# Gate and up weights in 1 MB pieces with 8 KB rows, and three transposing steps moved behind the modulation's sums, in a decoder block with 64 experts

## The chip, the cores and the metric

The kernel runs on one core of one Trainium2 chip. The metric is device time in microseconds from one launch. Three runs of the kernel before took 740.38, 738.90 and 739.66 us, median 739.66. A core has a matrix engine (TensorE, PE in the profile; PEld is its loading of the stationary operand), a vector engine (DVE), a scalar engine for activations (ACT), GpSimd (POOL), a queue engine (SP) that here issues nearly all loads, and 16 DMA engines that carry them from the chip's memory into the core's buffers.

## The reference, cut to what matters

One layer on 256 tokens of 1024 channels: modulation, two attention branches, then a mixture of 64 experts (8 for each token) and a shared expert, and a final norm. The parts that the change touches are the first modulation and the experts:

```python
mod = jax.nn.silu(c) @ w_ada[l] + b_ada[l]
shift1, scale1, gate1, shift2, scale2, gate2 = jnp.split(mod, N_MOD, axis=-1)
h = modulate(rms_norm(x, norm1_g[l]), shift1, scale1)
proj = h @ w_in[l]
...
def swiglu(x, w_gate, w_up, w_down):
    return (jax.nn.silu(x @ w_gate) * (x @ w_up)) @ w_down
...
def body(acc, bidx):                      # for every block of rows of one expert
    ye = swiglu(xt[rows], w_gate_e[e], w_up_e[e], w_down_e[e]) * wr[:, None]
    return acc.at[rows].add(ye.astype(acc.dtype)), None
...
return routed + swiglu(xt, w_gate_sh, w_up_sh, w_down_sh)
```

All is in 32 bit floats. An expert's gate and up matrices are 1024 x 256 (1 MiB each), its down matrix 256 x 1024 (1 MiB). All 64 experts are read: 192 MiB, which is 201 of the 266.73 MB that move.

## The kernel before

**Stages.** First the modulation row is summed (`mod_sums`, one step for each eighth of the channels, on TensorE, as its 1 MB of `w_ada` lands), and the normed tokens are turned so that channels lie on partitions (`turned`, four transposes of 128 x 128 a step, two channel blocks for both token tiles). `shift_scale` copies the sums out of PSUM on ScalarE, turns them into columns with four small products, and VectorE adds the biases. `modulated` makes the two parts (high and rest) of the modulated activations, `row_hi` and `row_lo` the two parts of the weights, and `proj_row` multiplies. Projections, both attentions and the output projection follow, then the router, and then the expert tiles.

**Expert tiles.** The experts are sorted by their number of tokens; the first six have fixed places. A tile has 128 slots: two experts of 64, one of 96 and one of 32, or four of 32. There are 26 tiles, 20 with two experts and 6 with four. For a tile TensorE gathers the tokens (`gather`), multiplies with gate and up weights (`tile_up`: the experts of a tile stand in column groups of the array, and their products run side by side), makes the slot map, adds the previous tile's result to the sums (`scatter`), turns the hidden activations and multiplies with the down weights (`down`). `swiglu` runs on ScalarE and VectorE meanwhile. Every product of 32 bit floats appears as two records in the trace.

**Weights.** They land in a ring of 20 buffers of 1 MiB (`w8()`; the names `w`, `vv`, `whi`, `wlo`, `hh`, `g2r`, `gr`, `sr`, `xs` in the rows are its buffers, most of them taken over from the attention stage). A buffer is handed out again when the tile that used it last is through with it. Loads are issued in program order by one queue on SP, which stops at a load whose buffer is not free or when earlier loads still have to land. In `load_gu` one buffer holds four of the eight channel blocks, gate and up of each: two loads of 512 KB, each row 4 KB. A tile loads the first half of all its experts and then the second. A down matrix is one load of 1 MB with 8 KB rows. The last tile's second halves come in pieces of 256 KB with 2 KB rows, and its down matrices in cuts of 512, 256 and 256 columns.

**Order.** The engines' programs are written out by hand (`plan`, `do`), so the order on every engine is that of the code.

Of the kernel before, what the change touches and what calls it, by code (L numbers as in the profile page):

```python
# [9 lines left out]
F32 = mybir.dt.float32  # L10
# [15 lines left out]
FF = 256  # L26
# [82 lines left out]
def block_kernel(ctx: ExitStack, tc: tile.TileContext, x, c, norm1_g, norm2_g, w_ada, b_ada, w_in,  # L109
                 w_branch_sb, w_branch_mb, w_out, w_router, router_bias, w_gate_e, w_up_e, w_down_e,  # L110
                 w_gate_sh, w_up_sh, w_down_sh, rel_bias, final_g, const_a, const_m, const_b, out):
    nc = tc.nc
# [47 lines left out]
    def load_gu(wg, wu, h):  # L160
        w = w8().rearrange("p (g j f) -> p g j f", g=2, j=4)
        nc.sync.dma_start(w[:, 0], wg.rearrange("(p j) f -> p j f", j=8)[:, 4 * h:4 * h + 4])
        nc.sync.dma_start(w[:, 1], wu.rearrange("(p j) f -> p j f", j=8)[:, 4 * h:4 * h + 4])
        return [w[:, :, j, :] for j in range(4)]
# [38 lines left out]
    with ExitStack() as pa:  # L203
# [158 lines left out]

        def shift_scale():

            sb = wk.tile([P, 512], F32, name="adasb", tag="ada", bufs=2)
            nc.scalar.activation(sb, rows.pop("m"), AF.Copy)
            p = big()
            firsts = ident.rearrange("p (n r) -> p n r", r=32)[:, :, 0]
            for k in range(4):
                mm(p[:, 4 * k:4 * k + 4], sb[:, 128 * k:128 * k + 128], firsts, start=True, stop=True,  # L370
                   skip_group_check=True)
            p = p[:, 0:16].rearrange("p (k i u) -> p i u k", k=4, i=2)
            m = modq.rearrange("p (u k) i -> p u k i", u=2)
            bq = biasq.rearrange("p (u k) i -> p u k i", u=2)
            nc.vector.tensor_tensor(m[:, :, :, 1], p[:, 0], bq[:, :, :, 1], op=OP.add)
            nc.vector.tensor_tensor(m[:, :, :, 0], p[:, 1], bq[:, :, :, 0], op=OP.add)
            nc.vector.tensor_tensor(modq[:, :, 2], modq[:, :, 0], gb[:, 0:8], op=OP.mult)
# [321 lines left out]
        for j in range(3, 8):  # L699
            if j > 3:  # L700
                do(turned, 2 * j - 8)
            do(mod_sums, j, keys=[("adk", j)])
        do(shift_scale)
        do(modulated, 0)
# [250 lines left out]
    def late_expert(k):  # L955
# [9 lines left out]
        gu = load_gu(wg, wu, 0) + load_gu(wg, wu, 1)  # L965
        wd = load_dn(wd)
        for first in (0, 128):
# [16 lines left out]
            for j in range(8):  # L984
                mm(p, xg[:, j], gu[j], start=j == 0, stop=j == 7)
# [5 lines left out]
    def load_shared():  # L991
        shw["gu"] = load_gu(w_gate_sh[0], w_up_sh[0], 0) + load_gu(w_gate_sh[0], w_up_sh[0], 1)
# [14 lines left out]
    def shared_up(t, j0, j1):  # L1007
        if j0 == 0:
            shp[t] = rot() if t else gub()
        for j in range(j0, j1):  # L1010
            mm(shp[t], h2T[0][:, j, t * 128:(t + 1) * 128], shw["gu"][j], start=j == 0, stop=j == 7)
# [76 lines left out]
    def load_tile(i):  # L1088
# [8 lines left out]
        if i == len(TILES) - 1:  # L1097

            gu = [load_gu(e[0], e[1], 0) for e in es]
            ws = [w8().rearrange("p (g j f) -> p g j f", g=2, j=4) for e in es]  # L1100
            for j in (0, 2):
                for w, e in zip(ws, es):
                    for g in range(2):
                        nc.sync.dma_start(w[:, g, j:j + 2],
                                          e[g].rearrange("(p j) f -> p j f", j=8)[:, 4 + j:6 + j])
            for g, w in zip(gu, ws):
                g += [w[:, :, j, :] for j in range(4)]
            return gu, load_dn_cuts([e[2] for e in es])
        gu = [[] for s in range(n)]
        for h in range(2):  # L1110
            for s in range(n):
                gu[s] += load_gu(es[s][0], es[s][1], h)
# [11 lines left out]
    def tile_up(i, xg, gu, between=()):  # L1124
        p = gub()
        for j in range(8):
            if j == 4:
                for f in between:
                    f()
            for c0, n, s in groups(i):  # L1130
                mm(p[c0:c0 + n, :], xg[:, j, c0:c0 + n], gu[s][j], start=j == 0, stop=j == 7, skip_group_check=True)  # L1131
# [203 lines left out]
```

## Time and profile before

| | |
|---|---|
| runs, median (three) | 739.66 us |
| profiled execution | 740.37 us, span of its instructions 738.6 us |
| TensorE busy | 691.3 us, 94% of the span |
| VectorE, ScalarE busy | 316.2 us (43%), 202.2 us (27%) |
| carried by DMA | 266.73 MB, mean 361 GB/s |
| gate and up loads | 512 KB each; down loads 1024 KB |

TensorE's records are pipelined, so a busy share of 94% does not say that it never waits: a wait shorter than a record's own length does not show as idle. The share of the DMA engines is the time their packets took over the time of 16 engines; it reads a little above 1 where every engine always has a packet, since one begins as the last ends. The chain of waits is followed back from the last instruction, so it shows for each stretch which resource ended last there. In the page's 40 slices the transfer rate is uneven until the fourteenth slice and then near 412 GB/s for most of the rest.

### The profile page before, as it was taken

To read this page: it belongs to the slowest core of one execution; us is meant where nothing else is said; L and a number is where in the kernel's file an instruction comes from. 1 tells how busy PE (TensorE), PEld (TensorE's weight loads), DVE (VectorE), ACT (ScalarE), POOL (GpSimd) and SP (SyncE) were. 2 spreads that over 40 slices of the span, in tenths; PEclk is the share of its full clock that TensorE was granted. 3 is DMA by queue.
4 is the path that set the end of the run, shared out by engine and by line. 5 is a ranking of instruction groups with operands and counts; after the bars stand their busy time and mean duration, and the time that the engine had idled before them with its cause. 6 is when DMAs were issued, how large, how long until landed. Compare 5 with 4: busy or idle time off the path is not lost.

```text
span 738.6 us, 12518 instructions
## 1 busy us (share of the span) xinstructions
PE 691.3 (94%) x4743; PEld 384.3 (52%) x4743; DVE 316.2 (43%) x667; ACT 202.2 (27%) x332; POOL 16.0 (2%) x33
## 2 busy tenths in 40 slices
PE   3899999999999999999999999999989998899994
PEld 0486677676888546444444454344444553355532
DVE  1366766666576833333333333233233332233323
ACT  2344666555835521111111111111111111111122
POOL 1010001000001000000000000000000000000000
PEclk9899999999999999999999999999999999999998
DMA  9999988777567699999999999999999999999994
GB/s 354 412 385 387 364 271 301 251 269 273 177 235 269 259 375 416 354 389 412 409 415 414 413 390 412 411 412 412 416 413 412 412 412 415 412 411 408 402 335 158
DMA packets 76862, 266.73 MB, mean 361 GB/s; under 512 B 7013, under 2 KB 9221, under 8 KB 67968
## 3 DMA queue, kind: packets, MB, share of 16 engines
q1 hardware_dynamic: 75344, 262.24, 91.7%
q0 software_dynamic: 1312, 3.65, 1.5%
q8 instruction: 39, 0.64, 0.4%
q14 instruction: 23, 0.19, 0.1%
q10 hardware_dynamic: 144, 0.00, 0.0%
HBM read 264.68 MB, written 1.19 MB: 360 GB/s over the span
## 4 chain that ended last, share of the span: by engine, by line
PE 51%; DMA 45%; DVE 2%; ACT 1%; issue 0%; SPq 0%; DVEq 0%; ACTq 0%
DMA w<-in_w_up_e_dram 17%; PE gu L1131 9%; PE big L272 7%; PE big L275 7%; PE big L273 7%; DMA wlo<-in_w_up_e_dram 7%; DMA sr<-in_w_down_e_dram 5%; PE rot L1155 4%; DMA w<-in_w_down_e_dram 4%; DMA hh<-in_w_down_e_dram 4%; DMA w<-in_w_ada_dram 4%; PE rot L1071 3%; DMA gr<-in_w_up_e_dram 3%; PE acc L1187 3%; PE att L420 2%; DMA hh<-in_w_gate_e_dram 2%
## 5 line engine op out<-in xcount | busy, mean ns | idle before, releaser
L1131 PE MATMUL gu<-w,hl 128*32 128x512 f32 (+1 forms) x568 | 99.0, 594 | 2.4 <-DMA w<-in_w_up_e_dram 2.0
L272 PE MATMUL big<-whi,hh 128*128 128x512 f32 x184 | 75.2, 409 | 1.7 <-ACT whi L392 1.7
L273 PE MATMUL big<-whi,hl 128*128 128x512 f32 x184 | 72.9, 396 | 0.0
L1004 DVE TENSOR_TENSOR sg<-sg,gu 128x256 f32<-128x256 f32 x27 | 11.4, 421 | 138.7 <-ACT sg L1003 138.7
L1071 PE MATMUL rot<-S,qksb 128*128 128x128 bf16 x624 | 69.1, 219 | 0.0
L1071 PE MATMUL rot<-S,qkmb 128*128 128x128 bf16 x624 | 68.7, 219 | 0.0
L1167 ACT ACTIVATE mg<-y 128x512 fp32r<-128x512 f32 x51 | 32.1, 629 | 130.2 <-DVE y L1161 130.2
L1161 DVE SCALAR_TENSOR_TENSOR y<-rot,wsl,gate 128x512 f32<-128x512 f32 (+1 forms) x53 | 39.1, 738 | 65.0 <-PE rot L1155 63.1
L1131 PEld LDWEIGHTS gu<-w,hl 128*32 128x32 f32 (+1 forms) x568 | 29.9, 121 | 60.9 <-issue 58.8
L1155 PE MATMUL rot<-w,at 128*32 128x512 f32 (+1 forms) x256 | 56.2, 610 | 5.7 <-DVE at L1019 5.7
L254 DVE TENSOR_TENSOR wlo<-w,whi 128x2048 fp32r<-128x2048 f32 x23 | 52.7, 2291 | 20.1 <-ACT whi L253 19.1
L275 PE MATMUL big<-wlo,hh 128*128 128x512 f32 x184 | 54.2, 395 | 0.2 <-DVE wlo L254 0.2
L1187 PE MATMUL acc<-mg,ST 128*128 128x512 f32 x204 | 54.0, 406 | 0.0
L1168 DVE TENSOR_TENSOR mg<-y,mg 128x512 fp32r<-128x512 f32 x51 | 35.3, 692 | 38.4 <-ACT mg L1167 38.4
L1075 ACT ACTIVATE hl<-rot 128x512 f32<-128x512 f32 x26 | 15.5, 597 | 120.8 <-PE rot L1071 120.8
L1003 ACT ACTIVATE sg<-gu 128x256 f32<-128x256 f32 x27 | 10.4, 383 | 138.5 <-PE gu L1131 138.5
L1071 PEld LDWEIGHTS <-qksb 128*128 128x128 bf16 x624 | 42.6, 98 | 7.8 <-issue 6.7
L1187 PEld LDWEIGHTS acc<-mg,ST 128*128 128x128 f32 x204 | 36.3, 188 | 17.4 <-ACT sg L1003 9.1
L253 ACT ACTIVATE whi<-w 128x2048 fp32r<-128x2048 f32 x23 | 43.9, 1909 | 5.0 <-PE big L273 5.0
L272 PEld LDWEIGHTS big<-whi,hh 128*128 128x128 f32 x184 | 35.1, 191 | 17.1 <-issue 3.8
L1071 PEld LDWEIGHTS <-qkmb 128*128 128x128 bf16 x624 | 43.6, 98 | 0.0
L275 PEld LDWEIGHTS big<-wlo,hh 128*128 128x128 f32 x184 | 34.8, 190 | 8.4 <-DVE wlo L254 0.6
(352 smaller groups left out, 1055.7 us busy)
## 6 DMA issues: line engine op xcount, KB each, us to landing
w<-in_w_gate_e_dram SPq DMA_DIRECT2D x60, 512.0 KB, 12.1
w<-in_w_up_e_dram SPq DMA_DIRECT2D x60, 512.0 KB, 12.6
w<-in_w_down_e_dram SPq DMA_DIRECT2D x26, 1024.0 KB, 12.5
w<-in_w_ada_dram SPq DMA_DIRECT2D x24, 1024.0 KB, 11.6
w<-in_w_in_dram SPq DMA_DIRECT2D x16, 1024.0 KB, 12.4
whi<-in_w_gate_e_dram SPq DMA_DIRECT2D x12, 512.0 KB, 11.3
whi<-in_w_up_e_dram SPq DMA_DIRECT2D x12, 512.0 KB, 11.7
wlo<-in_w_down_e_dram SPq DMA_DIRECT2D x6, 1024.0 KB, 11.3
```

Of the source, the lines that this page charges most:

```text
L253: nc.scalar.activation(hi, w, AF.Copy)
L254: nc.vector.tensor_tensor(lo, w, hi.bitcast(F32), op=OP.subtract)
L272: mm(p, aa[i][0], ww[i][0], start=start and i == 0, stop=False)
L273: mm(p, aa[i][1], ww[i][0], start=False, stop=False)
L275: mm(p, aa[i][0], ww[i][1], start=False, stop=stop and i == n - 1)
L1071: mm(p[:, b * 128:(b + 1) * 128], hp3[k // 3][k % 3][:, half * 4 + b, :], S[:, k // 3], start=k == 0, stop=k == 5)
L1131: mm(p[c0:c0 + n, :], xg[:, j, c0:c0 + n], gu[s][j], start=j == 0, stop=j == 7, skip_group_check=True)
L1155: mm(py[c0:c0 + w, 0:n], at[:, jj, c0:c0 + w], wd[s][:, jj, o:o + n], start=jj == 0, stop=jj == 1, skip_group_check=True)
L1161: nc.vector.scalar_tensor_tensor(y, py[:, 0:n], wsl, gate2[:, o:o + n], op0=OP.mult, op1=OP.mult)
L1167: nc.scalar.activation(yh, y, AF.Copy)
L1168: nc.vector.tensor_tensor(yl, y, yh.bitcast(F32), op=OP.subtract)
L1187: mm(sums(t, c), m if len(y) > 1 else m.bitcast(F32), part, start=False, stop=stop and k == len(y) - 1, skip_group_check=True)
```

## The change

Three edits. First, a gate matrix is one load of 1 MB into a buffer of its own and an up matrix another, each partition reading one row of 8 KB; a tile issues the gate loads of all its experts, then the up loads. In the last tile the up matrices come as 512, 256 and 256 KB. Second, the products follow: for every group first the eight gate products of 256 columns, then the eight up products (`up_cut`), where eight products of 512 columns stood. Third, at the front the steps `turned(2)`, `turned(4)` and `turned(6)` move from between the last sums to behind them, one beside the copy of the sums, two behind `shift_scale`; the copy is a step of its own (`mod_copy`).

```diff
-    def load_gu(wg, wu, h):
-        w = w8().rearrange("p (g j f) -> p g j f", g=2, j=4)
-        nc.sync.dma_start(w[:, 0], wg.rearrange("(p j) f -> p j f", j=8)[:, 4 * h:4 * h + 4])
-        nc.sync.dma_start(w[:, 1], wu.rearrange("(p j) f -> p j f", j=8)[:, 4 * h:4 * h + 4])
-        return [w[:, :, j, :] for j in range(4)]
+    def load_gu(wg, wu):
+
+        ws = [w8().rearrange("p (j f) -> p j f", j=8) for _ in range(2)]
+        for w, d in zip(ws, (wg, wu)):
+            nc.sync.dma_start(w, d.rearrange("(p j) f -> p j f", j=8))
+        return ws
+
+    def up_cut(p, xg, gu, gs, k):
+
+        g, j = divmod(k, 8)
+        for c0, n, s in gs:
+            mm(p[c0:c0 + n, FF * g:FF * g + FF], xg[:, j, c0:c0 + n], gu[s][g][:, j, :], start=j == 0, stop=j == 7,
+               skip_group_check=True)
...
+        def mod_copy():
+            sb = rows["c"] = wk.tile([P, 512], F32, name="adasb", tag="ada", bufs=2)
+            nc.scalar.activation(sb, rows.pop("m"), AF.Copy)
+
         def shift_scale():
 
-            sb = wk.tile([P, 512], F32, name="adasb", tag="ada", bufs=2)
-            nc.scalar.activation(sb, rows.pop("m"), AF.Copy)
-            p = big()
+            sb, p = rows.pop("c"), big()
...
         for j in range(3, 8):
-            if j > 3:
-                do(turned, 2 * j - 8)
+            if j == 4:
+                do(turned, 0)
             do(mod_sums, j, keys=[("adk", j)])
+
+        do(mod_copy)
+        do(turned, 2)
         do(shift_scale)
+        do(turned, 4)
+        do(turned, 6)
         do(modulated, 0)
...
-        for j in range(j0, j1):
-            mm(shp[t], h2T[0][:, j, t * 128:(t + 1) * 128], shw["gu"][j], start=j == 0, stop=j == 7)
+        for k in range(2 * j0, 2 * j1):
+            up_cut(shp[t], h2T[0][:, :, t * 128:(t + 1) * 128], [shw["gu"]], [(0, 128, 0)], k)
...
-            gu = [load_gu(e[0], e[1], 0) for e in es]
-            ws = [w8().rearrange("p (g j f) -> p g j f", g=2, j=4) for e in es]
-            for j in (0, 2):
-                for w, e in zip(ws, es):
-                    for g in range(2):
-                        nc.sync.dma_start(w[:, g, j:j + 2],
-                                          e[g].rearrange("(p j) f -> p j f", j=8)[:, 4 + j:6 + j])
-            for g, w in zip(gu, ws):
-                g += [w[:, :, j, :] for j in range(4)]
+            gu = [[w8().rearrange("p (j f) -> p j f", j=8) for g in range(2)] for e in es]
+            for g, o, m in ((0, 0, 8), (1, 0, 4), (1, 4, 2), (1, 6, 2)):
+                for w, e in zip(gu, es):
+                    nc.sync.dma_start(w[g][:, o:o + m], e[g].rearrange("(p j) f -> p j f", j=8)[:, o:o + m])
             return gu, load_dn_cuts([e[2] for e in es])
-        gu = [[] for s in range(n)]
-        for h in range(2):
-            for s in range(n):
-                gu[s] += load_gu(es[s][0], es[s][1], h)
+        gu = [[w8().rearrange("p (j f) -> p j f", j=8) for g in range(2)] for e in es]
+        for g in range(2):
+            for w, e in zip(gu, es):
+                nc.sync.dma_start(w[g], e[g].rearrange("(p j) f -> p j f", j=8))
         return gu, [load_dn(e[2]) for e in es]
...
         p = gub()
-        for j in range(8):
-            if j == 4:
+        for k in range(16):
+            if k == 8:
                 for f in between:
                     f()
-            for c0, n, s in groups(i):
-                mm(p[c0:c0 + n, :], xg[:, j, c0:c0 + n], gu[s][j], start=j == 0, stop=j == 7, skip_group_check=True)
+            up_cut(p, xg, gu, groups(i), k)
```

What the edits do to the order is read best from the engines' own programs. At the front, TensorE before: line 360 is a sum, line 351 a transposing step (`att<-ca,gr`), line 370 the products that turn the sums into columns, line 272 the first projection product.

```order
L360 MATMUL big<-w_112,cpad 32x512 x4
L351 MATMUL att<-ca,gr_102 128x128 x4
L360 MATMUL big<-w_114,cpad 32x512 x4
L351 MATMUL att<-ca,gr_102 128x128 x4
L360 MATMUL big<-w_116,cpad 32x512 x4
L351 MATMUL att<-ca,gr_102 128x128 x4
L360 MATMUL big<-w_118,cpad 32x512 x4
L351 MATMUL att<-ca,gr_102 128x128 x4
L360 MATMUL big<-w_125,cpad 32x512 x4
L370 MATMUL big<-ca,adasb 128x4 x4
L272 MATMUL big<-whi,hh 128x512
```

The same place on TensorE after the change (sums are line 368 now, steps 359, columns 380, products 280):

```order
L368 MATMUL big<-w_112,cpad 32x512 x4
L359 MATMUL att<-ca,gr_102 128x128 x4
L368 MATMUL big<-w_114,cpad 32x512 x4
L368 MATMUL big<-w_116,cpad 32x512 x4
L368 MATMUL big<-w_118,cpad 32x512 x4
L368 MATMUL big<-w_125,cpad 32x512 x4
L359 MATMUL att<-ca,gr_102 128x128 x4
L380 MATMUL big<-ca,adasb 128x4 x4
L359 MATMUL att<-ca,gr_102 128x128 x8
L280 MATMUL big<-whi,hh 128x512
```

The sums stand together now, one transposing step behind them and two behind the columns.

The loads' queue on SP at tile 2 before (two fixed experts; the name ahead of the arrow is the ring's buffer, and the order is hh, g2r, gr, gr):

```order
L162 DMA hh<-in_w_gate_e_dram 128x1024
L163 DMA hh<-in_w_up_e_dram 128x1024
L162 DMA g2r<-in_w_gate_e_dram 128x1024
L163 DMA g2r<-in_w_up_e_dram 128x1024
L162 DMA gr_2449<-in_w_gate_e_dram 128x1024
L163 DMA gr_2449<-in_w_up_e_dram 128x1024
L162 DMA gr_2452<-in_w_gate_e_dram 128x1024
L163 DMA gr_2452<-in_w_up_e_dram 128x1024
L168 DMA sr<-in_w_down_e_dram 128x2048
L168 DMA xs<-in_w_down_e_dram 128x2048
```

The same tile in SP's queue after:

```order
L1122 DMA hh<-in_w_gate_e_dram 128x2048
L1122 DMA gr_2483<-in_w_gate_e_dram 128x2048
L1122 DMA g2r<-in_w_up_e_dram 128x2048
L1122 DMA gr_2484<-in_w_up_e_dram 128x2048
L176 DMA sr<-in_w_down_e_dram 128x2048
L176 DMA xs<-in_w_down_e_dram 128x2048
```

Half as many loads of twice the size, and the buffers of a tile are asked for in the order first, third, second, fourth.

## Rows read from the trace of the kernel before

**Rows 1.** The page: chain that ended last, shares of the span by engine.

```profile
PE 51%; DMA 45%; DVE 2%; ACT 1%; issue 0%; SPq 0%; DVEq 0%; ACTq 0%
```

**Rows 2.** That chain in order of time: start us, length us, what.

```profile
338.60 12.52 DMA w<-in_w_down_e_dram
...
641.92 3.62 PE gu L1131 x14
...
712.44 8.29 DMA hh<-in_w_down_e_dram
720.74 5.84 DMA hh<-in_w_down_e_dram
```

**Rows 3.** Timeline, TensorE: first up product of four tiles (start, length, instruction).

```profile
597.48 0.60 PE L1131 MATMUL gu<-w,hl 128*64 128x512 f32 x2
...
614.30 0.63 PE L1131 MATMUL gu<-w,hl 128*32 128x512 f32 x3
...
635.19 0.64 PE L1131 MATMUL gu<-xs,hl 128*64 128x512 f32 x1
...
655.23 0.60 PE L1131 MATMUL gu<-w,hl 128*64 128x512 f32 x2
```

**Rows 4.** Windows: stretch, us, busy us of five engines, clock, DMA share, GB/s.

```profile
351.00:369.00 18.00, 17.48 (x186) 8.03 (x178) 5.83 (x15) 2.24 (x4) 0.00 (x0) 1.00 1.03 408
601.00:615.00 14.00, 13.48 (x106) 6.92 (x106) 4.30 (x11) 1.61 (x3) 0.00 (x0) 1.00 1.03 409
371.00:379.00 8.00, 7.49 (x90) 5.02 (x86) 2.77 (x8) 0.98 (x2) 0.00 (x0) 1.00 1.02 421
```

**Rows 5.** Waits of the loads' queue, 300 to 345 us: total, times, longest.

```profile
SPq L162 <- PE rot L1155: 7.6, 2, 7.3
```

**Rows 6.** Line 162, 340 to 695 us: its register instruction, one for each load.

```profile
L162 SPq FUSED_REGOPS  x92: 37/42/56, 341.3 to 689.2; - x92
```

**Rows 7.** The window in which the last tile's small pieces move.

```profile
698.00:712.00 14.00, 13.48 (x121) 6.86 (x120) 4.73 (x9) 1.86 (x3) 0.20 (x1) 1.00 0.93 328
```

**Rows 8.** Tile 2 on the timeline, then two groups by form (busy, mean ns).

```profile
301.44 3.60 PE L1131 MATMUL gu<-gr,hl 128*64 128x512 f32 x16
...
305.11 0.60 PE L1141 MATMUL rot<-qkmb,ca 64*64 64x256 f32 x4
...
L1131 PE MATMUL gu<-gr,hl 128*64 128x512 f32 x64 | 21.4, 592 | 0.0
...
L1141 PE MATMUL rot<-qkmb,ca 64*64 64x256 f32 x64 | 9.5, 376 | 0.0
```

**Rows 9.** Timeline of the loads' queue: two gate pieces of tile 2.

```profile
243.94 0.33 SPq L162 DMA_DIRECT2D g2r<-in_w_gate_e_dram  x1
...
255.87 0.33 SPq L162 DMA_DIRECT2D gr<-in_w_gate_e_dram  x1
```

**Rows 10.** Timeline, TensorE, 20 to 33 us, idle time in brackets.

```profile
20.17 1.94 PE L360 MATMUL big<-w,cpad 128*32 128x512 f32 x8
...
23.91 0.66 PE L351 MATMUL att<-ca,gr 128*128 128x128 f32 x4
...
27.23 1.07 PE L360 MATMUL big<-w,cpad 128*32 128x512 f32 x8 [0.85 <-DMA w<-in_w_ada_dram]
29.01 1.45 PE L370 MATMUL big<-ca,adasb 128*128 128x4 f32 x8 [0.72 <-ACT adasb L366]
32.11 0.79 PE L272 MATMUL big<-whi,hh 128*128 128x512 f32 x1 [1.65 <-ACT whi L392]
```

**Rows 11.** Windows at the front, columns as in rows 4.

```profile
26.09:29.50 3.41, 1.84 (x16) 0.69 (x14) 0.00 (x0) 0.60 (x1) 0.00 (x0) 1.00 1.02 408
32.92:36.33 3.41, 3.41 (x8) 2.48 (x8) 3.38 (x7) 2.64 (x6) 0.00 (x0) 0.50 1.02 408
36.33:39.75 3.42, 3.42 (x16) 2.79 (x15) 3.35 (x8) 2.06 (x4) 0.17 (x1) 1.00 1.04 389
```

**Rows 12.** Loads of the stationary block by form: count, busy us, mean ns.

```profile
L1131 PEld LDWEIGHTS gu<-w,hl 128*64 128x64 f32 x232 | 17.8, 137 | 36.6 <-issue 34.8 <-DMA w<-in_w_gate_e_dram 0.6 <-DVE hl L1077 0.6
```

More of the change, by code (lines that the diff above doesn't have):

```diff
@@ L964, in late_expert @@
         wg, wu, wd = (w[0, bass.ds(ev, 1)].rearrange("o a b -> (o a) b") for w in (w_gate_e, w_up_e, w_down_e))
-        gu = load_gu(wg, wu, 0) + load_gu(wg, wu, 1)
+        gu = load_gu(wg, wu)
         wd = load_dn(wd)
@@ L983, in late_expert @@
             p = gub()
-            for j in range(8):
-                mm(p, xg[:, j], gu[j], start=j == 0, stop=j == 7)
+            for k in range(16):
+                up_cut(p, xg, [gu], [(0, 128, 0)], k)
             at = hidden_T(swiglu(p))
@@ L991, in load_shared @@
     def load_shared():
-        shw["gu"] = load_gu(w_gate_sh[0], w_up_sh[0], 0) + load_gu(w_gate_sh[0], w_up_sh[0], 1)
+        shw["gu"] = load_gu(w_gate_sh[0], w_up_sh[0])
     def load_shared_down():
@@ L1125, in tile_up @@
         p = gub()
-        for j in range(8):
-            if j == 4:
+        for k in range(16):
+            if k == 8:
                 for f in between:
                     f()
-            for c0, n, s in groups(i):
-                mm(p[c0:c0 + n, :], xg[:, j, c0:c0 + n], gu[s][j], start=j == 0, stop=j == 7, skip_group_check=True)
+            up_cut(p, xg, gu, groups(i), k)
         return swiglu(p)
```

## The prediction, made before the changed kernel ran

> **What bounds the kernel now.** I read the chain of work that ended last first. By engine it is split almost evenly between TensorE and DMA [rows 1], so neither can be called the bound before one sees where each stands. In order of time [rows 2] the chain runs on TensorE until about 338 us, then it is DMA landings of expert weights until 642, then TensorE again until 712, and the last two steps are landings of the last tile's down weights; what follows the last one at 726.62 is some 12 us of closing arithmetic (738.6 less 726.6), which nothing here touches.
>
> Second, I looked at how close the two are. A tile that nothing delays takes 16.8 us on TensorE (597.48 to 614.30), while the next two take 20.89 and 20.04 [rows 3]; 4.1 + 3.3 = 7.4 us of that is waiting for weights. So TensorE works without a pause for long stretches, and only at the tiles of four experts, which bring twice the bytes, does it run dry. Meanwhile the 16 DMA engines show a share of 1.02 or 1.03 in the three windows read there [rows 4]: they are the resource with no slack, and what they carry per microsecond sets when the last weights land. Before about 345 us it is the other way round: the queue that issues the loads waits for TensorE to free a buffer [rows 5].
>
> So a microsecond saved on the DMA engines after 345 us is a microsecond at the end, as long as TensorE keeps up; a microsecond saved on TensorE before 338 frees buffers earlier and moves everything behind it.
>
> **Part one: rows of 8 KB for the gate and up weights.** Every gate and up piece was 512 KB with 4 KB rows and becomes 1 MB with 8 KB rows, which is the form that the down weights have already. The trace therefore has both prices. In two windows in which only 4 KB rows moved the engines carried 408 and 409 GB/s; in one in which only down weights moved, 421 at the same share [rows 4]. One MiB (1.049 MB) takes 2.567 us at 408.5 and 2.491 us at 421: 0.076 us less. From 341 us on, the line that issues gate pieces for full tiles ran 92 times [rows 6], with as many up pieces beside it, so 92 MiB change form in the stretch that counts: 92 x 0.076 = 7.0 us. The window with 8 KB rows is 8 us long, and one row more or less on half of the engines (0.07 MB of 3.4) moves its rate by 2%, so a good part of the difference could be chance: at 418 it would be 5.4 us, at 424 8.6. I take 7.0.
>
> **Part two: the last tile.** Its second 4 MiB came in sixteen 256 KB pieces of 2 KB rows. The 14 us in which they were issued and carried show 328 GB/s at a share of 0.93 [rows 7]: 14 x 0.328 = 4.6 MB, for which 11.2 us would have done at 408.5, so 2.8 us were lost. Half of these bytes now come as 512 KB pieces, and eight small pieces remain. If the loss goes with the small pieces, half of it (1.4) returns; if it belongs to the down pieces of 2 KB and 1 KB rows queued behind them, nothing does; 2.8 is the other end. I take 1.0.
>
> **Part three: gate products first.** Each tile issues twice as many products of half the width, so each stationary block is loaded twice. The steps now: 16 records, which are eight steps of two groups each, in 3.60 us, of which 0.59 is the last record's own length, so seven steps take 3.01, 0.43 us a step at 512 columns [rows 8]. Two groups of 64 at 256 columns occur in the same tile's slot map: four records, two steps, end 0.60 us after the first began, of which 0.38 is one record's own length, so a step is 0.22 [rows 8]. A tile's 32 steps take 32 x 0.22 = 7.0 us where 16 x 0.43 = 6.9 stood: 0.1 to 0.2 more at the rounding of these rows, nothing at the least. After 345 us the 7.4 us of waits at two tiles cover it. In the few tiles before 338 us and in the shared expert's two products it is on the chain: I take 0.3, between 0 and 1.0. The activation of the gate half could start sooner, but its result is waited for only behind other work of the same tile, so it counts nothing.
>
> **Part four: the order of the loads.** All gate pieces of a tile are issued before the first up piece, while the buffers are still handed out expert by expert. So an up piece now stands in the queue behind a gate piece whose buffer comes free later. The order rows show it at the third tile: the piece into hh is followed by one into gr, and the one into g2r comes after. Before, g2r was issued at 243.94 and gr had to wait until 255.87 [rows 9]; now g2r waits with gr, and 1 MiB that moved in those 12 us moves later. That costs 2.6 us if nothing hides it. Almost all of it is hidden, because the queue waits 7.6 us for TensorE between 300 and 345 anyway [rows 5] and the deferred megabyte is carried there. I take 0.5, between 0 and 2.6.
>
> **Part five: three transposing steps behind the sums.** The last modulation sum starts at 27.23 after 0.85 us of waiting for its weights, so taking three steps of transposes out of its way does not make it earlier [rows 10]. Behind it TensorE idles 0.72 us for the copy and 1.65 us for the first converted weights. One step (0.66) fits the first hole; two fit the second, 1.3 us at the rate of that row. At the slower rate, by the ratio of two sums (1.94 to 1.07), two steps take 2.4, so the first projection product begins at 32.11 or at most 0.7 later. What can move is the clock. Up to 36.33 it was granted at 0.50 (1.2 GHz), some time after a stretch in which TensorE was busy 1.84 of 3.41 us, and at 1.00 (2.4 GHz) afterwards [rows 11]. With the holes filled it may return by 32.92: the 3.41 us of products there would take half, a gain of 1.7. On the other side, TensorE now has less to do between 22 and 27 us, and if the clock falls sooner the last sum takes 1.94 instead of 1.07 [rows 10]: a loss of 0.9. I weigh the gain at four in ten (0.4 x 1.7 = 0.7), the loss at two in ten (0.2), and the rest at a loss of 0.1: a gain of some 0.4. TensorE is on the chain from there to 338, so it passes on whole.
>
> **Sum.** 7.0 + 1.0 + 0.4 - 0.3 - 0.5 = 7.6 us less. The profiled execution took 740.37 us, 1.8 more than its span, and would become 732.8. It was the slowest of the three runs shown, 0.7 above their median of 739.66; on the median the forecast is 732.1. TensorE allows it: at the wait of tile 635.19 some 76 of the 92 MiB have been carried, so weights come 76 x 0.076 = 5.8 us earlier, less than the 7.4 us of waits; 1.6 remain. From there its own chain ends about as much earlier as the last landings do.
>
> **Rivals.**
> *TensorE becomes the bound, and the kernel is slower.* The mechanism is the doubled loading of stationary blocks. A load of 64 columns is shown with 137 ns [rows 12]. If each of a tile's 16 added steps waited for its load rather than having it under the stream, the tile would take 16 x 0.137 = 2.2 us more; 25 tiles make 55 us, less the 7.4 of waits that it would fill: 740 + 48 = 788. The last of those waits stands behind 21 tiles, so it decides from 7.4/21 = 0.35 us a tile, 0.022 of each added step. Against it: the 0.22 us step above has these very loads in it. The Trainium skill has a rule for it (TensorE: Matmul & The Clock Gate, Back-to-back issue gap): in a stream of load and matmul pairs the spacing is set by both, 81 ns at 128 columns. By that rule, which gives the sign of this rival, the step would be longer than its columns; the row just named does not show it.
> *The rate does not rise.* If something behind the engines set 409 GB/s, part one is worth nothing: 739.66 - 1.0 - 0.4 + 0.8 = 739.1, no change. For it: the share stands above 1 in both forms. Against it: 421 in the same buffers [rows 4]. The Trainium skill (DMA: Bandwidth & Descriptors, SWDGE vs HWDGE vs iDMA) puts a packet preferably at no more than 4096 B, by which a longer row would be cut and gain nothing; the trace's faster windows speak against it.
> *Half is given back as waits.* The in-order queue stands for a later buffer more often when TensorE has no slack, and the engines idle. Half of part one: 735.6. For it: the waits of rows 5; against it: the share above 1 in all three windows of rows 4, where the same queue fed the engines.
> *More than the sum:* the clock returns early and the last tile's small pieces cost less: 730.
>
> **Numbers.** Forecast 0.62 (its own range 730.5 to 734.5), more 0.14, half given back 0.15, no rise 0.06, TensorE bound 0.03. All bounds at their good end give 727, all at the bad end without the rivals 739; the range for 8 in 10 is 729 to 737. A measurement of this kernel can tell about 0.2%, 1.5 us, from no change. Faster than that: 0.62 + 0.14 + 0.15, less a little for sums gone wrong: 0.89; same 0.07; slower 0.04.
>
> **What would show it.** Right: windows of pure gate or up pieces at 420 GB/s; two-expert tiles still at 16.8 us; waits at the two late tiles shorter by 5 to 6 us; the last landing near 719. Wrong: tiles of 17.3 us or more (part three); a share below 1 with a free TensorE (part four); the sums at 1.94 us after 24 us, or a first projection product after 32.5 (part five); 409 GB/s as before (part one).

## The result and the profile after

The changed kernel took 729.95 us in the median of four runs (728.64 to 732.79), the kernel before 739.28 in four beside them: ratio 0.9878, 95% interval 0.9846 to 0.9911. That is 9.3 us less by the medians, between 6.6 and 11.4 by the interval. Timed again in five runs it took 730.53, ratio 0.9872 (0.9849 to 0.9896). The forecast, 7.6 us less or a ratio of 0.9897, lies inside the first interval and just outside the second. The profiled execution took 730.29 us with a span of 728.4.

The chain that ended last, by engine and in order of time (start, length), answers [rows 1, 2]:

```profile
PE 82%; DMA 12%; DVE 3%; ACT 1%; issue 1%; SPq 0%; DVEq 0%; ACTq 0%
```

```profile
569.78 2.51 PE rot L1086 x45
572.29 19.76 DMA w<-in_w_down_e_dram
592.18 20.46 DMA hh<-in_w_up_e_dram
612.76 19.63 DMA w<-in_w_up_e_dram
632.43 3.67 PE gu L171 x30
...
710.08 1.96 PE rot L1164 x16
```

From 338 to 642 us the chain had been weights landing but for 7.5 us at 551; now three landings of expert weights stand in it, from 572 to 632, and from 29 us on nearly all the rest is TensorE. No landing of down weights ends it any more: the last cut's products, which had to wait until 726.62, start at 714.97, right behind TensorE's own work.

The same on TensorE's timeline (start, length, instruction, idle time before it in brackets): the first up product of four tiles and the wait between them, as in [rows 3].

```profile
593.53 0.82 PE L171 MATMUL gu<-w,hl 128*64 128x256 f32 x6
...
610.38 0.41 PE L171 MATMUL gu<-w,hl 128*32 128x256 f32 x2
...
627.27 0.43 PE L171 MATMUL gu<-xs,hl 128*64 128x256 f32 x1
...
632.43 0.43 PE L171 MATMUL gu<-w,hl 128*64 128x256 f32 x1 [1.06 <-DMA w<-in_w_up_e_dram]
...
645.78 0.39 PE L171 MATMUL gu<-w,hl 128*64 128x256 f32 x2
```

The tiles take 16.85, 16.89 and 18.51 us where 16.82, 20.89 and 20.04 stood. One wait is left, 1.7 us against the undisturbed tile.

Windows (busy us of five engines, clock, DMA share, GB/s), for [rows 4] and [rows 7]:

```profile
351.00:369.00 18.00, 17.48 (x262) 10.46 (x258) 5.70 (x14) 2.24 (x4) 0.00 (x0) 1.00 1.02 420
601.00:615.00 14.00, 13.48 (x166) 8.26 (x166) 5.56 (x12) 1.92 (x4) 0.00 (x0) 1.00 1.01 420
371.00:379.00 8.00, 7.48 (x85) 4.79 (x87) 2.83 (x7) 0.77 (x2) 0.00 (x0) 1.00 1.02 420
...
698.00:712.00 14.00, 12.48 (x146) 6.51 (x142) 2.36 (x6) 3.02 (x5) 0.00 (x0) 1.00 0.98 340
```

Gate, up and down weights now move at the same 420 GB/s, and the share is still above 1. How many packets the bytes of the first window came in, before and after:

```profile
DMA packets 2008, 7.34 MB, mean 408 GB/s; under 512 B 223, under 2 KB 223, under 8 KB 2005
```

```profile
DMA packets 1036, 7.56 MB, mean 420 GB/s; under 512 B 115, under 2 KB 115, under 8 KB 115
```

A row is one packet, and the traces' records of single packets give its price: one of 4096 B took 163.4 ns in the mean (351 to 369 us before), one of 8192 B 314.7 ns (371 to 379 us before; 314.8 in the first window after). Two short ones take 326.8, 12 ns more than one long one.

At the front (timeline as above, then windows), for [rows 10, 11]:

```profile
24.62 1.07 PE L368 MATMUL big<-w,cpad 128*32 128x512 f32 x8 [0.84 <-DMA w<-in_w_ada_dram]
27.13 1.94 PE L368 MATMUL big<-w,cpad 128*32 128x512 f32 x8 [1.45 <-DMA w<-in_w_ada_dram]
...
32.68 0.50 PE L280 MATMUL big<-whi,hh 128*128 128x512 f32 x1 [0.72 <-ACT whi L402]
```

```profile
23.37:26.78 3.41, 1.48 (x12) 0.16 (x8) 0.00 (x0) 0.00 (x0) 0.00 (x0) 1.00 1.00 413
26.78:30.20 3.42, 3.07 (x14) 1.33 (x15) 0.00 (x0) 0.60 (x1) 0.00 (x0) 0.50 1.04 413
30.20:33.60 3.40, 2.65 (x17) 1.89 (x17) 1.83 (x6) 2.06 (x5) 0.00 (x0) 1.00 1.03 407
```

With the transposes gone TensorE was busy 1.48 of 3.41 us and the clock fell to 1.2 GHz at 26.78, sooner than before; the last sum took 1.94. But it was back at 2.4 GHz by 30.20 instead of 36.33, so the projection's products run at full clock from the first one.

### The profile page after: what moved, and what is told of

It reads as the page before. It is cut to its first block, busy times and chain, and to the rows that moved or that the text cites. A ratio compares the mean times of both kernels' runs of the same rounds, so it can differ in the third digit from the quotient of the medians.

```text
span 728.4 us, 14362 instructions
## 1 busy us (share of the span) xinstructions
PE 684.1 (94%) x5927; PEld 443.4 (61%) x5927; DVE 316.4 (43%) x667; ACT 202.4 (28%) x332; POOL 16.0 (2%) x33
## 4 chain that ended last, share of the span: by engine, by line
PE 82%; DMA 12%; DVE 3%; ACT 1%; issue 1%; SPq 0%; DVEq 0%; ACTq 0%
PE gu L171 23%; PE rot L1164 11%; PE rot L1086 8%; PE big L280 7%; PE big L283 7%; PE big L281 7%; PE acc L1196 7%; DMA w<-in_w_ada_dram 4%; DMA hh<-in_w_up_e_dram 3%; DMA w<-in_w_down_e_dram 3%; DMA w<-in_w_up_e_dram 3%; PE att L430 2%; PE rot L1150 2%; DVE at L1034 1%; PE acc L1050 1%; PE rot L1031 1%
## 5 line engine op out<-in xcount | busy, mean ns | idle before, releaser
L171 PE MATMUL gu<-w,hl 128*32 128x256 f32 (+1 forms) x1136 | 114.4, 380 | 1.5 <-DMA w<-in_w_up_e_dram 1.1
L171 PEld LDWEIGHTS gu<-w,hl 128*32 128x32 f32 (+1 forms) x1136 | 67.6, 121 | 42.4 <-issue 5.0
L1019 DVE TENSOR_TENSOR sg<-sg,gu 128x256 f32<-128x256 f32 x27 | 11.4, 421 | 132.1 <-ACT sg L1018 132.1
L171 PE MATMUL gu<-whi,hl 128*64 128x256 f32 (+1 forms) x208 | 46.4, 380 | 0.0
## 6 DMA issues: line engine op xcount, KB each, us to landing
w<-in_w_in_dram SPq DMA_DIRECT2D x16, 1024.0 KB, 12.5
```

Source lines behind the costliest of these rows:

```text
L171: mm(p[c0:c0 + n, FF * g:FF * g + FF], xg[:, j, c0:c0 + n], gu[s][g][:, j, :], start=j == 0, stop=j == 7, skip_group_check=True)
```

## The experiments

All ratios are to the kernel before, run on the same chip beside them. One more measure is used: the time from the first up product of the first expert tile to that of the tile behind TensorE's last wait for weights, **the stretch**. It was 655.23 less 261.21 = 394.0 before and 645.78 less 260.40 = 385.4 after. It holds the weights' stream and leaves the front and the tail out. The experiments ran in three groups on three chips, in which the kernel before took 739.23 us (front, rows), 739.48 (changed again, last tile, fewer bytes, 128 columns) and 738.75 (buffers, late product, both, 128 columns with fewer loads) in the median.

**The changed kernel again**, without an edit.

> The changed kernel itself, unaltered, timed in more rounds beside the others. Theory: 730.0, ratio 0.988 with an interval of less than 0.002 to each side. Where a profile has a fall of the clock to 1.2 GHz between 270 and 280 us the first full tile comes 1.6 us later, and since TensorE is the limit to the end these 1.6 us stay in the time. Rival: the four times first measured were lucky in the clock, 731.5, ratio 0.990.

730.53, ratio 0.9872 (0.9849 to 0.9896), stretch 385.4 again. The rival's 0.990 lies just above the interval, so the first four runs were not lucky by that much. The fall of the clock at 271.85 is tied to nothing in the change: it stands in the profile of before and, at 273.13, in one of the experiments that have the new front (fewer bytes, below), and in none of the others, the old front taken back included; how often it comes with either front, no run shows. Where it stands, the next tile starts 15.06 or 15.08 us after the second half of the first expert tile's up products instead of 13.43. So 1.6 of the 8.6 us between the two stretches are this fall, and 7.0 are left. The changed kernel's profile has a fall at 538.78, right behind 1.5 us in which TensorE was idle, and it costs as much (20.64 for a tile that takes 18.92 without it). This one is more than chance: it stands near 538 in the repetition too and in five of the experiments (front taken back, front alone, two 512 KB pieces, last tile, buffers), and not in the profile of before, which has the same idle time there.

**Length of the rows, or number of pieces?**

```diff
 # 1 MB pieces, rows of 4 KB
-                nc.sync.dma_start(w[g], e[g].rearrange("(p j) f -> p j f", j=8))
+                nc.sync.dma_start(w[g].rearrange("p (h j) f -> p h j f", h=2),
+                                  e[g].rearrange("(h p j) f -> p h j f", h=2, j=4))
 # two 512 KB pieces, rows of 4 KB
-                nc.sync.dma_start(w[g], e[g].rearrange("(p j) f -> p j f", j=8))
+                for o in (0, 4):
+                    nc.sync.dma_start(w[g][:, o:o + 4], e[g].rearrange("(p j) f -> p j f", j=8)[:, o:o + 4])
```

> The changed kernel, but each 1 MB piece of gate and up weights for full tiles takes its rows from two places of the matrix, so that it moves in rows of 4 KB; number, size and order of the pieces, the buffers and the products are as in the changed kernel (the products use other rows of the weights than they should). Theory, the length of the rows is what counts: the rate over 350 to 600 us falls back to 409 GB/s, some 85 MiB cost 0.076 us more each, 6.5 us, of which TensorE's remaining slack hides none: 736.5 (735 to 738). Rival, the number and size of pieces counts (half as many issues and completions): the rate stays at 420 and the time at 730.

> The changed kernel, but each 1 MB piece of gate and up weights for full tiles is loaded as two pieces of 512 KB with rows of 4 KB, one behind the other, into the same buffer; the products are as in the changed kernel. Theory, the length of the rows: 409 GB/s and 736.5 (735 to 738), the same as with 1 MB pieces of 4 KB rows. Rival, number of pieces: 409 GB/s here and 420 with the 1 MB pieces of 4 KB rows. Rival, the gain came from the order of the products and from whole buffers: 730 here.

737.42, ratio 0.9977 (0.9965 to 0.9989), and 737.46, ratio 0.9980 (0.9966 to 0.9993): twelve runs each, and no difference between them. The windows of 1 MB pieces with 4 KB rows, then of the halves:

```profile
351.00:369.00 18.00, 17.48 (x258) 10.49 (x254) 5.70 (x14) 2.24 (x4) 0.00 (x0) 1.00 1.03 410
```

```profile
351.00:369.00 18.00, 17.48 (x258) 10.31 (x254) 5.70 (x14) 2.24 (x4) 0.00 (x0) 1.00 1.03 411
```

Everything else of the change is in both, and both lose 6.9 us of it, against the 730.53 of the changed kernel in another group. The waits come back too; with 1 MB pieces and 4 KB rows:

```profile
616.69 0.62 PE L171 MATMUL gu<-wlo,hl 128*32 128x256 f32 x2 [1.95 <-DMA wlo<-in_w_up_e_dram]
...
619.23 0.64 PE L171 MATMUL gu<-hh,hl 128*32 128x256 f32 x1 [1.92 <-DMA hh<-in_w_up_e_dram]
```

The stretch is 392.0 and 390.8, so 5.4 to 6.6 us of the 6.9 lie in the stream. It is the length of the rows; size and number of the pieces are worth nothing that these runs tell. What both keep, 1.8 us below the kernel before beside them by the medians and 1.5 to 1.7 by the ratios, is what all the rest of the change is worth together.

**The front, taken back and alone.**

```diff
 # taken back, in the changed kernel; "alone" is the reverse edit in the kernel before
-            if j == 4:
-                do(turned, 0)
+            if j > 3:
+                do(turned, 2 * j - 8)
...
-        do(turned, 2)
         do(shift_scale)
-        do(turned, 4)
-        do(turned, 6)
```

> The changed kernel with the three transposing steps put back between the modulation sums; the weights stay in 1 MB pieces with 8 KB rows. Theory: of the 9.3 us measured, the front gave 0.8 by the start of the first experts (261.21 to 260.40), and TensorE now sets the end nearly everywhere, so undoing it gives back that much: 730.8, ratio to the changed kernel 1.001, with the clock at 1.2 GHz again near 30 to 36 us and the first projection product near 32.1. Rival, more from the front: the clock's fall at 271.85 us, which the profile of the kernel before shows and that of the changed kernel does not, belongs to the front too; then 2.4 come back: 732.4, ratio 1.003. Rival, nothing from the front: 730.0, ratio 1.000, and the first experts start at 260.4 all the same.

> The kernel before with the three transposing steps behind the sums, and its weights as they were (512 KB pieces with 4 KB rows, gate and up side by side). Theory: the front is worth 0.8 us at the first experts, and since landings of weights set the end from 340 us on, what arrives at the end is at most that: 738.5 to 739.3. Rival, more from the front: 2.4 us by way of the clock near 272 us as well: 736.9. Rival, the front alone explains what the forecast missed: 737.6 (1.7 less).

Taken back: 731.13, ratio 0.9901 (0.9879 to 0.9923). Alone: 737.52, ratio 0.9997 (0.9977 to 1.0018). The times do not agree on an effect of this size. Alone, the median is 1.7 us below the 739.23 of before, near what the rival with 737.6 gave, but four of its twelve runs took 739 to 743 us, and the ratio gives 0.2. Taken back, it is 0.6 by the medians and 2.1 by the ratios (0.9901 less 0.9872). So the traces have to say it. With the front taken back the last sums take 1.07 and 1.06 us, the first projection product starts at 31.57, and the clock is at 1.2 GHz in the same window as in [rows 11]:

```profile
32.92:36.33 3.41, 3.41 (x9) 2.64 (x10) 3.34 (x8) 2.58 (x7) 0.00 (x0) 0.50 1.05 414
```

The first experts then start at 261.57; alone, the new front lets them start at 260.36. The rows that end the front, taken back and alone:

```profile
261.57 0.65 PE L171 MATMUL gu<-w,hl 128*64 128x256 f32 x4
```

```profile
260.36 1.08 PE L1138 MATMUL gu<-w,hl 128*64 128x512 f32 x4
```

Over all profiles (but the two of 128 columns below, whose shared expert comes before it and takes longer) the old front gives 261.21 and 261.57, the new one 259.25 to 260.80, and 262.42 once, when the clock stood at 1.2 GHz for 10 us. The middle of the ten with the new front is 260.4: 1.0 us earlier than the two of the old. The starts go with the time at 1.2 GHz near 30 us: 259.25 to 259.58 in the three profiles without any, 260.36 to 260.51 in the four with some 3.4 us of it, 260.76 and 260.80 with 6.8, 262.42 with 10; the old front had 6.8 us in both. The stretch is the same 385.4 with either front, so this microsecond reaches the end whole. The rival with 2.4 us falls as told: neither of these two profiles has a fall near 272 us.

**The last tile.**

```diff
-            for g, o, m in ((0, 0, 8), (1, 0, 4), (1, 4, 2), (1, 6, 2)):
+            for g, o, m in ((0, 0, 8), (1, 0, 8)):
```

> The changed kernel with the up weights of the last tile in four pieces of 1 MB too (gate pieces are so already), in place of four of 512 KB and eight of 256 KB. Theory: TensorE's own chain sets the end (in the changed kernel's trace the second half of the last tile's products starts at 704.39 behind other work of TensorE, not behind a landing), the small pieces cost the transfers about 1 us, and that is worth nothing at the end: 730.0, between 729.5 and 731.0 if the fourth expert's whole piece lands a little behind 704.4. Rival, the small pieces still cost the end what they cost the transfers: 729.0 or less. Rival, the pieces are needed: the products of the fourth expert wait for a whole piece that lands 2.5 us later than the first small one: 732.5.

730.31, ratio 0.9872 (0.9849 to 0.9895): the same. Its window over the tail:

```profile
698.00:712.00 14.00, 12.48 (x150) 6.38 (x142) 2.36 (x6) 3.17 (x5) 0.00 (x0) 1.00 0.92 328
```

Without one small up piece the share stays at 0.92 and the rate at 328 GB/s. But at one time the kernels are at different pieces. The stretches with a share below 1, before, after and with whole pieces:

```profile
700.00:714.00 14.00, 13.48 (x98) 5.68 (x99) 4.53 (x9) 2.68 (x5) 0.20 (x1) 1.00 0.93 314
```

```profile
692.00:704.00 12.00, 11.48 (x105) 5.36 (x104) 4.05 (x8) 2.04 (x4) 0.04 (x1) 1.00 0.86 308
```

```profile
702.00:711.00 9.00, 7.48 (x82) 3.53 (x84) 0.85 (x2) 2.86 (x4) 0.00 (x0) 1.00 0.91 311
```

By the packets' sizes it is mainly small pieces of gate and up that move in the first two and down cuts in the third, so the loss goes with neither kind alone; why it comes is open. The last 8 MB of weights took 24.4 us before, 23.1 to 25.3 in the profiles with the new last tile and 23.3 with whole pieces. It decides nothing at the end, since TensorE is last.

**Buffers in the order of issue; the late product; both.**

```diff
 # buffers
-        gu = [[w8().rearrange("p (j f) -> p j f", j=8) for g in range(2)] for e in es]
+        gu = [[w8().rearrange("p (j f) -> p j f", j=8) for e in es] for g in range(2)]
+        gu = [list(w) for w in zip(*gu)]
 # late product: past_capacity keeps its key in a dead buffer and ends there; the rest is a step of the next tile
-             SH_AT + 4: [past_capacity]}
+             SH_AT + 4: [past_capacity], SH_AT + 5: [past_ranks]}
+    def past_ranks():
+        p = rot()
+        mm(p[0:1, 0:NE], ca[0:NE, C_KEY + NE + 1:C_KEY + NE + 2], keyr, start=True, stop=True)
+        ...
```

> The changed kernel with the buffers of a full tile handed out in the order in which its pieces are issued (all gate pieces, then all up pieces), so that no up piece stands behind a gate piece whose buffer comes free later. Theory, the deferred megabyte of part four costs the transfers up to 2.5 us before 300 us and is visible only as TensorE's last wait for weights: with it gone that wait of 1.4 us shrinks or goes, 728.6 to 729.5. Rival, it is hidden wholly: 730.3 as the changed kernel, with the wait near 630 us as long as before.

> The changed kernel with the last product of the step that looks for experts over capacity (and the store of its result) moved one tile later, so that TensorE does not idle for 1.8 us (535.91 to 537.70 in the changed kernel's trace) behind VectorE's chain; the clock falls to 1.2 GHz right there in that trace (538.78 to 542.20) and a tile there takes 20.64 us, where one without the fall took 18.92. Theory, two limits side by side: TensorE comes up to 3.4 us earlier to the tile at 627 and waits there that much longer for weights that land when they did: 730.0 (729.5 to 730.5), the wait 1.4 + 3.4 = 4.8 us. Rival, TensorE alone is the limit: 726.7 to 728.3.

> Both of the foregoing edits: buffers in the order of issue, and the late product one tile later. Theory, two limits side by side: earlier transfers let the earlier TensorE through, so the two together are worth more than the sum of each: 727 to 728. Rival, TensorE alone: as with the late product alone. Rival, transfers alone: as with the buffers alone.

Buffers: 729.52, ratio 0.9877 (0.9855 to 0.9898), stretch 385.4, the last wait 1.1 us as before. The rival holds: the deferred megabyte was hidden wholly.

Late product: 730.56, ratio 0.9894 (0.9874 to 0.9914). TensorE does come 3.1 us earlier to the tile that stood at 610.38, and waits that much longer. Its waits for weights from 606 to 635 us:

```profile
613.16 0.40 PE L171 MATMUL gu<-hh,hl 128*32 128x256 f32 x1 [1.75 <-DMA hh<-in_w_up_e_dram]
628.05 0.43 PE L171 MATMUL gu<-w,hl 128*64 128x256 f32 x1 [0.76 <-DMA w<-in_w_gate_e_dram]
633.03 0.43 PE L171 MATMUL gu<-w,hl 128*64 128x256 f32 x1 [1.30 <-DMA w<-in_w_up_e_dram]
```

3.8 us instead of 1.06 (the theory had 4.8), and a stretch of 385.6: the transfers set it, and the rival falls. Both edits: 727.79, ratio 0.9861 (0.9839 to 0.9883), stretch 384.2. That is the theory's time, and the fastest of the versions that load all weights, but its interval overlaps that of the changed kernel, and why both together shorten the stretch by 1.1 us where neither does alone is not settled.

**Fewer bytes.**

```diff
+            for s, (w, e) in enumerate(zip(gu, es)):
+                if g == 1 and s == 3:
+                    w[1] = w[0]
+                    continue
```

> The changed kernel without the load of the fourth expert's up weights in the five full tiles of four experts (its products use the gate weights instead): 5 MiB less to move, 12.5 us of the engines at 421 GB/s; buffers, products and everything else are as in the changed kernel. Theory, TensorE sets the end: only its last wait for weights (1.4 to 1.7 us at the tile that starts at 627.27) goes, 728.3 (727.5 to 729). Rival, the transfers still set the end: most of the 12.5 us comes off, 718 to 721.

726.31, ratio 0.9824 (0.9800 to 0.9848): 4.2 us less than the changed kernel, not 12.5. In this profile TensorE waits for no weights from 260 us on. All that it waits for from 600 to 650 us (total, times, longest) is VectorE:

```profile
PE rot L1167 <- DVE at L1034: 1.5, 3, 0.5
```

So TensorE's own chain ends a few microseconds below the transfers. The theory named the limit rightly and put the gain some 2 us too low: it left out the fall near 538, which this profile does not have (18.93 for that tile instead of 20.64). Without waits for weights the time is TensorE's, and goes with its clock: the profiled execution took 730.42, 4.1 above the median, with 10 us at 1.2 GHz at the front and the fall at 273.13, yet no fall near 538. Which falls the other runs had, no profile shows.

**Products of 128 columns, and these with fewer loads.** In both, the sums of two halves are open at once in one accumulation buffer, and the sums are not those of the reference; number and size of the products are what is looked at.

```diff
 # 128 columns
-            mm(p[c0:c0 + n, FF * g:FF * g + FF], xg[:, j, c0:c0 + n], gu[s][g][:, j, :], start=j == 0, stop=j == 7,
-               skip_group_check=True)
+            for h in (0, 128):
+                mm(p[c0:c0 + n, FF * g + h:FF * g + h + 128], xg[:, j, c0:c0 + n], gu[s][g][:, j, h:h + 128],
+                   start=j == 0, stop=j == 7, skip_group_check=True)
 # fewer loads, in addition
+                if g == 1:
+                    w[1] = w[0]
+                    continue
```

> The changed kernel with each gate and up product cut once more, into two of 128 columns, so that each stationary block is loaded twice as often again. Theory, the columns set the step as long as the loads are shorter than the stream: the step was 0.43 us at 512 columns and 0.216 at 256, and at 128 it would be 0.108, with 64 steps a tile again 6.9 us; but a load of 64 columns is shown with 0.137 us and one of 32 with 0.106 to 0.124, longer than this. So theory: the step becomes 0.137, the tile 16.8 + 64 x 0.029 = 18.7, and 25 tiles with the shared expert's two make 50 us: 780 (760 to 800). Rival, loads of one group lie beside another group's stream and never show: 730 to 733.

> The changed kernel with products of 128 columns and without any load of up weights for full tiles (the products use the gate weights twice), some 60 MiB less to move. With 128 columns and all loads the time was 749, and TensorE stood seven times for 1.6 to 2.0 us after 340 us with no work of another engine to wait for, each time right behind a 16 KB piece of program that arrived about 6 us after the one before. Theory, the program's pieces come late because the weights fill the engines: with a third fewer weights the pauses go, and without waits for weights the time is 749 less 12 to 14: 735 to 737. Rival, pieces of program come at a pace of their own, whatever else moves: the pauses stay, 746 to 748.

748.99, ratio 1.0120 (1.0098 to 1.0143): neither 780 nor 733. The step is set by the columns, as the rival had it; two steps of one group in a tile of two experts:

```profile
443.83 0.27 PE L172 MATMUL gu<-hh,hl 128*64 128x128 f32 x1
443.84 0.32 PE L172 MATMUL gu<-gr,hl 128*64 128x128 f32 x1
443.94 0.27 PE L172 MATMUL gu<-hh,hl 128*64 128x128 f32 x1
```

0.11 us from 443.83 to 443.94, half of the 0.22 at 256 columns, and the tile takes 16.98 us; the stationary blocks' loads do not show. What costs the time is something that neither theory had: TensorE stands 1.5 to 1.8 us in the middle of a tile with nothing that it waits for ("issue"), as here in a tile of four groups, which takes 18.87.

```profile
369.68 5.62 PE L172 MATMUL gu<-w,hl 128*32 128x128 f32 x194
376.89 1.35 PE L172 MATMUL gu<-w,hl 128*32 128x128 f32 x40 [1.59 <-issue]
```

With a third fewer weights to move the time is 747.04 in five runs (a sixth took 754.05), ratio 1.0100 (1.0069 to 1.0130), and the pauses before products of line 172 still sum to 7.8 us (8.2 with all loads; with those before other lines 11.2 and 11.3). The engines' share from 340 to 420 us is down to 0.79, so the theory that weights crowd the program out falls; the rival's time is right, its fixed pace is not shown.

## Why the prediction was right, step by step

**What bounds it.** Right, and closer than it said. The transfers carried the end, TensorE had 7.4 us of waits at the two late tiles and keeps 1.8 (0.1 at 610.38, 1.7 at 627.27). The forecast left 1.6 there and named waits shorter by 5 to 6 us: 5.6. That this came out so closely is in part luck. The working had TensorE run dry at these two tiles only, but the trace of before has waits for weights at two earlier ones:

```profile
530.30 0.59 PE L1131 MATMUL gu<-sr,hl 128*32 128x512 f32 x1 [0.86 <-DMA sr<-in_w_up_e_dram]
...
550.74 3.62 PE L1131 MATMUL gu<-w,hl 128*64 128x512 f32 x14 [0.53 <-DMA w<-in_w_up_e_dram]
```

These tiles took 20.77 and 18.33 us where 18.92 and 16.84 stand without a wait, 3.3 us more that the sum left out; against it the fall at 538.78 takes 1.7 us of TensorE's margin in the changed kernel's profile, and without it the waits were 3.8 (late product). The late product and the fewer bytes show both limits: TensorE 3 us faster brings nothing, transfers 12.5 us shorter bring 4.

**Part one, 7.0.** Right. The two kernels with 4 KB rows lose 6.9 us in the medians and 7.8 to 8.0 by the ratios (0.0105 and 0.0108 of 739.3). The rate went from 408 to 420 GB/s as the one window with 8 KB rows had it, so that window of 8 us was not chance; the packets' own times, 326.8 ns for two of 4096 B and 314.7 for one of 8192 B, are the mechanism. The Trainium skill prefers packets of at most 4096 B, in a table on the transfers that GpSimd issues (DMA: Bandwidth & Descriptors, SWDGE vs HWDGE vs iDMA); here loads from SP's queue with longer rows moved 3% more in the same time at the same share, and the measurement decides.

**Part two, 1.0.** Not seen. The window went from 328 to 340 GB/s, but it holds other pieces after than before, and the last 8 MB took as long as before (24.4 us, then 23.1 to 25.3). Since the last tile no longer waits for a landing, what the transfers gain there is worth nothing at the end either. The forecast took the bound of nothing for the case that the loss belongs to the down pieces; nothing was right, the reason is not shown.

**Part three, a loss of 0.3.** Right. A tile of two experts takes 16.76 us where 16.72 stood, 25 tiles 1.0 us of TensorE. Of this the end sees what stands on the chain: 0.1 in the shared expert (19.97 us from its first product to the first experts, 19.87 before), 0.1 in the four tiles up to 346 us (67.98, 67.86) and 0.1 in the three behind 645.78 (51.04, 50.92), 0.3 in all; in between the stream sets the time.

**Part four, a loss of 0.5.** Nothing: buffers in the order of issue leave the stretch at 385.4. The wait for TensorE between 300 and 345 us that was to hide it [rows 5] is still there after:

```profile
SPq L1122 <- PE rot L1164: 7.0, 1, 7.0
```

**Part five, a gain of 0.4.** Too small: 1.0 by the starts of the first experts. The step that was mis-sized is the weighing of gain (1.7) and loss (0.9) as cases that exclude one another. Both came in one execution: the last sum took 1.94, and the clock was back at 30.20. Both signs of being wrong that were named, a sum at 1.94 after 24 us and a first projection product after 32.5 (32.68), came true; they showed the loss and hid the gain, since the products behind them ran at full clock: the place to look was the end of the front. In three of the ten profiles with the new front the clock did not fall at the front at all.

**The sum.** 7.0 + 1.0 + 0.4 - 0.3 - 0.5 = 7.6 against 9.3 measured, with 6.6 to 11.4 possible. By the experiments: rows 6.9 to 8.0, front 1.0, part three some 0.3 the other way, the rest near nothing: 7.6 to 8.7. The two kernels with 4 KB rows put all but the rows at 1.5 to 1.8 together, which makes 8.4 to 9.8. What is left to 9.3 is within what the runs tell. One sign did not come as named: the last weights landed at 714.1 by the records of packets, where 726.1 stood and 719 was forecast; 1.6 us of these 12.0 are the fall at 271.85 in the profile of before.

**The rivals.** TensorE as the bound by doubled loads did not come: the loads stay under the stream even at 128 columns. A rate that stays: refuted by 420. Half given back: refuted by a share above 1 and by part four. More than the sum: the time was the 730 that this rival gave, just below the forecast's own range (730.5 to 734.5); of its two reasons the early clock came, and the last tile's small pieces brought nothing.

## What to carry to other kernels

Where the DMA engines show a share of 1 without a break, look for a stretch in which only one kind of row moves and compare its rate with the others': the price of a layout stands there before it is changed. Before counting a gain, find how far behind the second limit stands (here 1.7 us of TensorE), since beyond it neither engine's microseconds are worth anything alone. When a step's cost is uncertain because of the clock, look at where the work ends, not at where its first instruction stands.

## What the runs showed of the hardware that was not expected

TensorE seems to run out of program. With 8295 records of products instead of 5927 the program came in 67 pieces instead of 48, two of them in the 12 us of the pause shown above (rows of DMA queues: packets, MB, share; of that window, then of the whole page of the changed kernel):

```profile
q8 instruction: 2, 0.03, 1.1%
```

```profile
q8 instruction: 48, 0.79, 0.4%
```

The pauses of 1.5 to 1.8 us fall where products are shortest and most (tiles of four groups, 256 records in some 7 us). Each of the seven ends 1.3 to 1.5 us after a piece has landed: the one above at 376.89, behind a piece that was there at 375.60. With fewer loads it is 1.2 to 1.5. So they are very probably waits for program; no run made the program shorter at the same products. The Trainium skill (Runtime: NRT & Kernel Launch, Instruction fetch mechanics) has the fetch of such a piece mostly hidden: at 256 columns the trace agrees, at 128 it does not.
